# Two small experts in one shared float32 block, and modulation vectors from six wide groups

## Chip, core and metric

The kernel runs on one core of one Trainium2 chip (trn2). The metric is device time in microseconds (us), from the start to the end of one execution; three runs were taken and their median counts. A row says PE for TensorE, PEld for its weight loads, DVE for VectorE, ACT for ScalarE, POOL for GpSimd and SP for SyncE, whose queue issues nearly all transfers here.

## What is computed

One inference step over two transformer layers on 384 tokens: 128 context tokens and 256 latent tokens, width 1024, all in float32. Cut to what matters:

```
shift_a, scale_a, gate_a, shift_f, scale_f, gate_f = split(silu(cond) @ ada_w + ada_b, 6)
h = LN(x) * (1 + scale_a) + shift_a
x = LN1(alpha * x + gate_a * mixers(h))          # attention, short convolution, chunk MLP
h = LN(x) * (1 + scale_f) + shift_f
x = LN2(alpha * x + gate_f * ffn(h))
ffn, layer 0: (silu(h @ w1) * (h @ w3)) @ w2      # d_ff 2816
ffn, layer 1: top 2 of 8 experts, each the same form with d_ff 1408, gated and summed
```

`cond` is one vector for the context tokens and one for the latent tokens, so a modulation vector has two versions. The 6 x 1024 outputs of `ada_w` per layer are counted here in 12 blocks `nb` of 512 columns: 0 to 3 are shift_a and scale_a, 4 and 5 gate_a, 6 to 9 shift_f and scale_f, 10 and 11 gate_f.

Routing the reference's inputs gives 159, 70, 117, 54, 63, 126, 57 and 122 tokens to experts 0 to 7 (768 in all).

## The kernel before

Precision: a product of two float32 matrices is split. Each operand is a high part (`float32r`, cast by ACT) and a rest (`x - high`, subtracted by DVE), and `mm3` issues three fast matmuls: high x high, high x rest, rest x high. A weight block of 1 MB arrives in one of five staging buffers (tag `st`), is cast and subtracted in two halves (`split`, `split2`) into tiles `wh` and `wl`, and the staging buffer is free again once DVE has subtracted. A plain float32 matmul needs no split, and the profile shows it as two records.

Order: all work is recorded by a planner (`Plan`), which gives every instruction a price (`price`), keeps data dependences, buffers and an estimated time for each engine, and writes out the order of each engine; where PE would sit idle for long it inserts filler matmuls (`keep_warm`, line 510; they read only `idr`). All planned instructions carry line 493 or 495 (495: the further matmuls of a bundle that `matmuls` keeps together).

Modulation: `ada_rows` loads 2 MB of `ada_w` for a block `nb` and runs 16 records of 32-row matmuls, four at a time in four column groups of PE, into one PSUM bank, whose four row groups hold partial sums. They are copied into a high part and a rest and summed by matmuls with a 0/1 matrix: `ada_cols` turns them into columns (8 small matmuls with `selc`), `ada_bcast` into rows on all 128 partitions (4 matmuls with `selb`), and `ada_dram` writes two rows to DRAM (2 matmuls with `selc`), from where `spread` broadcasts them by DMA. Start: 4 blocks; mixers of layer 0: 6; dense FFN: 6; mixers of layer 1: 8. In all 48 MB.

Experts (`moe`): expert 7 comes first, since its number is known while routing is not; `order_list` then puts an expert with more than 128 tokens last. `expert` returns ten steps: gate and up matmuls (`up`, in column blocks of 512, 512 and 384), `prep`, `down`, `end`. A block holds up to 128 tokens, gathered by an indirect DMA, transposed on PE and split. Expert 7 and the seven others make eight full blocks. The last one carries a second block of 32 tokens, which is not split and runs in four column groups (`small`). Per full block: 162 matmuls with 512 columns and 48 with 384, and 17.3 MB of weights. `scatter` adds the blocks' results to the tokens, 12 matmuls per block, after the blocks 0 to 2, 3 and 4, and 5 and 6. Tokens beyond these blocks would go to `further` blocks, under a condition at run time, each a whole expert with its loads.

PSUM: eight banks, three tagged `pd` (up matmuls), two `py` (down matmuls, modulation), three `pm`.

## Time and profile before

| | |
|---|---|
| Runs | 1173.18, 1175.70, 1180.41 us; median 1175.7 |
| Profiled execution | 1172.83 us, of which the span from first to last instruction is 1171.1 |
| PE busy | 1133.1 us, 97% of the span |
| DVE, ACT, POOL busy | 827.2, 626.4, 124.3 us |
| Moved by DMA | 282.66 MB, on average 241 GB/s |

A row of a window gives, for a stretch of the span, its length, the busy time of each engine with its number of instructions, the clock granted to PE as a share of full speed, the busy share of the DMA engines and what they moved. PE's busy time comes from modelled ends of pipelined matmuls: of two neighbours the distance of the starts tells the pace, not the length of one. In a timeline, rows of one kind are merged, with their count behind an x.

### The profile page before, as it was taken

To read this page: it belongs to the slowest core of one execution; us is meant where nothing else is said; L and a number is where in the kernel's file an instruction comes from. 1 tells how busy PE (TensorE), PEld (TensorE's weight loads), DVE (VectorE), ACT (ScalarE), POOL (GpSimd) and SP (SyncE) were. 2 spreads that over 40 slices of the span, in tenths; PEclk is the share of its full clock that TensorE was granted. 3 is DMA by queue.
4 is the path that set the end of the run, shared out by engine and by line. 5 is a ranking of instruction groups with operands and counts; after the bars stand their busy time and mean duration, and the time that the engine had idled before them with its cause. 6 is when DMAs were issued, how large, how long until landed. Compare 5 with 4: busy or idle time off the path is not lost. (4 is left out here: it accounts for less than half of the span.)

```text
span 1171.1 us, 15554 instructions
## 1 busy us (share of the span) xinstructions
PE 1133.1 (97%) x5578; PEld 862.3 (74%) x5578; DVE 827.2 (71%) x1391; ACT 626.4 (53%) x997; POOL 124.3 (11%) x141
## 2 busy tenths in 40 slices
PE   8999999999999999989999899999999999999995
PEld 4666668877777878756666677888888888887673
DVE  4475669443535344797568877999999998987855
ACT  4545547431313223264455326878878786885652
POOL 3430003000000000055000110000000000011201
PEclk8999999999999999999999969999999999999998
DMA  9775544573839465354557436999979997996541
GB/s 375 275 267 197 166 142 143 199 269 139 328 110 332 150 238 197 149 185 156 199 186 268 163 130 224 352 362 361 345 294 347 379 361 297 366 343 245 184 176 58
DMA packets 49398, 282.66 MB, mean 241 GB/s; under 512 B 6312, under 2 KB 8104, under 8 KB 21408
## 3 DMA queue, kind: packets, MB, share of 16 engines
q1 hardware_dynamic: 47056, 275.46, 63.7%
q0 software_dynamic: 1392, 4.55, 1.1%
q10 hardware_dynamic: 864, 1.57, 0.4%
q8 instruction: 46, 0.75, 0.3%
q14 instruction: 40, 0.33, 0.1%
HBM read 278.13 MB, written 3.43 MB: 240 GB/s over the span
## 5 line engine op out<-in xcount | busy, mean ns | idle before, releaser
L493 PE MATMUL bank<-q,q 128*128 128x512 f32 (+4 forms) x4111 | 969.6, 389 | 2.6 <-DVE q L493 1.3
L493 PEld LDWEIGHTS bank<-q,q 128*128 128x128 f32 x4111 | 734.4, 189 | 196.4 <-issue 33.6
L493 DVE TENSOR_TENSOR q<-st,q 128x1024 fp32r<-128x1024 f32 x394 | 453.9, 1178 | 113.4 <-ACT q L493 89.0
L493 ACT CAST q<-st 128x1024 fp32r<-128x1024 f32 x394 | 394.0, 1016 | 196.0 <-PE bank L493 101.3
L493 DVE TENSOR_TENSOR q<-bank,q 128x512 fp32r<-128x512 f32 (+5 forms) x117 | 73.0, 635 | 70.6 <-ACT q L493 57.7
L493 DVE TENSOR_TENSOR q<-q,bank 128x512 f32<-128x512 f32 (+3 forms) x111 | 63.8, 584 | 76.7 <-PE bank L493 69.9
L493 ACT CAST q<-bank 128x512 fp32r<-128x512 f32 (+2 forms) x97 | 53.7, 562 | 103.7 <-PE bank L493 94.0
L493 ACT COPY q<-bank 128x128 f32<-128x128 f32 (+3 forms) x184 | 54.5, 350 | 76.3 <-PE bank L493 67.9
L493 PE MATMUL bank<-idf,q 128*128 128x128 f32 (+1 forms) x502 | 81.7, 287 | 12.9 <-ACT q L493 7.4
L493 POOL TENSOR_TENSOR q<-q,nhalf 128x1 f32<-128x1 f32 (+3 forms) x42 | 42.0, 1005 | 473.8 <-DVE q L493 473.7
L493 PEld LDWEIGHTS bank<-idf,q 128*128 128x128 f32 (+1 forms) x502 | 63.2, 147 | 39.5 <-ACT q L493 12.6
L493 POOL TENSOR_TENSOR q<-q,q 128x512 fp32r<-128x512 f32 (+5 forms) x69 | 61.5, 909 | 216.6 <-ACT q L493 155.0
L493 ACT ACTIVATE q<-bank 128x512 f32<-128x512 f32 (+4 forms) x57 | 29.6, 520 | 81.2 <-PE bank L493 74.4
L493 DVE TENSOR_TENSOR q<-q,q 128x512 f32<-128x512 f32 (+13 forms) x131 | 52.3, 420 | 17.4 <-POOL q L493 8.5
L493 PE MATMUL bank<-st,cs 128*32 128x512 f32 x384 | 54.8, 606 | 0.3 <-DMA st<-in_ada_w_dram 0.3
L272 POOL DMA_INDIRECT q<-dr,q x9 | 14.7, 1638 | 346.3 <-DVE q L493 346.3
L493 ACT ACTIVATE q<-bank,q 128x384 f32<-128x384 f32 (+2 forms) x62 | 33.5, 551 | 24.6 <-DVE q L493 21.5
L493 DVE TENSOR_REDUCE q<-bank 128x1 f32<-128x384 f32 (+5 forms) x64 | 24.5, 411 | 20.8 <-PE bank L495 13.5
L493 DVE SCALAR_TENSOR_TENSOR q<-q,q,q 128x512 f32<-128x512 f32 (+1 forms) x43 | 35.5, 882 | 0.1
L510 PE MATMUL bank<-idr 128*128 128x512 f32 x85 | 30.3, 500 | 1.9 <-DVE selt L667 1.7
L495 PE MATMUL bank<-q,q 64*128 64x384 f32 (+2 forms) x76 | 31.7, 515 | 0.0
L493 ACT ACTIVATE q<-bank,q,q 128x128 f32<-128x128 f32 x70 | 26.6, 467 | 4.6 <-DVE q L493 2.8
(90 smaller groups left out, 395.4 us busy)
## 6 DMA issues: line engine op xcount, KB each, us to landing
st<-in_ada_w_dram SPq DMA_DIRECT2D x48, 1024.0 KB
st<-in_moe_w2a_dram SPq DMA_DIRECT2D x40, 1024.0 KB
st<-in_moe_w1a_dram SPq DMA_DIRECT2D x32, 1024.0 KB
st<-in_moe_w3a_dram SPq DMA_DIRECT2D x32, 1024.0 KB
st<-in_ffn_w_dram SPq DMA_DIRECT2D x22, 1024.0 KB
st<-in_w_in_dram SPq DMA_DIRECT2D x16, 1024.0 KB
st<-in_moe_w1b_dram SPq DMA_DIRECT2D x16, 768.0 KB
st<-in_moe_w3b_dram SPq DMA_DIRECT2D x16, 768.0 KB
```

The lines of the kernel that those rows point to most:

```text
L272: self.nc.gpsimd.indirect_dma_start(out=out, out_offset=None, in_=src.rearrange("p t d -> (p t) d"), in_offset=o)
L493: getattr(self.real[o.eng], o.name)(*a, **k)
L495: getattr(self.real[o.eng], o.name)(*[x.real() for x in b], **q)
L510: self.nc.tensor.matmul(z, a, b, start=True, stop=True)
```

## The change

1. The experts other than 7 are sorted by their number of tokens, inside the kernel (`order_list`). Ranks 1 to 4 and then 0 are full blocks as before, so there are six full blocks, not eight. Ranks 5 and 6, the two smallest, share one block (`gather_pair`, `pair`): 64 tokens each, in the two column halves of PE, in plain float32, straight from the staging buffers. Its work is 18 steps (gate and up in halves of the contraction, down in halves), which `PLACES` spreads between the steps of the other blocks, from step 7 to the last block's start. Each half step loads 1 MB (or 0.75 or 0.5) for each of the two experts. `scatter` now runs after the blocks 0 and 1, 2 and 3, 4 and the pair. The loads stay at eight experts.
2. Modulation: four blocks `nb` are done together, in their own column groups, so that a bank holds finished sums and not partial ones: `ada_group` accumulates over eight loads of 1 MB, `ada_out` copies the bank once, transposes it on PE (4 transposes for four blocks) and adds the bias, or adds it to two rows and writes them to DRAM. All gates now come by `spread`. `selc` and `selb` are gone (only the start keeps 8 matmuls with a small 0/1 matrix `selk`). Start: 8 MB as before; mixers of layer 0: 16 MB (12 before); dense FFN: 8 (12 before); mixers of layer 1: 16. In the FFN the bank of a group is held from the second to the fifth column block.
3. Prices of PE in the planner: a fast 512-column matmul from 214 to 232, the smallest fast one from 54 to 112, others by a few ns. `further` gets one more possible block (`MAXX`), and its list is made earlier.

```diff
-MAXX = 5
+MAXX = 6
 W = 32
+
+
+RANKS = (1, 2, 3, 4, 0)
+PAIR = (5, 6)
+H = P // 2
+
+PLACES = (4, 7, 56)
...
-CAPS2 = dict(a4=8, wh=6, wl=6)
-FILL0 = ((0,),(1,),(2,3),())
-GATE = 1
+CAPS2 = dict(a4=10, wh=6, wl=6)
...
-                return 57 if ins[0].dt == F32R else 107
+                return 62 if ins[0].dt == F32R else 109
...
-                return max(54, n * 0.4167 + 1 if n >= 256 else n * 1.6667 + 1)
+                return max(112, n * 0.4453 + 4)
             half = o.cells.shape[0] == 2 or ins[0].cells.shape[0] == 2
-            return max(107, n * (0.85 if half else 1.6667) + 3)
+            return max(214 if len(ins)>1 else 107, n * (0.85 if half else 1.6667) + 6)
...
+    def ada_group(self, l, n, units, zr=None):
+
+
+        nc = self.nc
+        zr = zr or self.bank([512], name="zrows", tag="py")
+        for u in units:
+            w = self.load(self.A["ada_w"][l, n, u], 4, 512)
+            split = (l, n) == (0, 0)
+            first, last = (u % 4 == 0, u % 4 == 3) if split else (u == 0, u == KC - 1)
+            k = [4 * (j % 2) + u % 4 if split else u for j in range(4)]
+            nc.matmuls([(zr[32 * j : 32 * j + 32, :], self.cs[:, k[j], :], w[:, j, :], dict(start=first, stop=last, tile_position=(0, 32 * j))) for j in range(4)])
+        return zr
...
+    def ada_out(self, l, n, zr, cols, rows):
+
+        nc = self.nc
+        if cols:
+            e = self.m2([512], name="ae")
+            nc.any.copy(e, zr)
+            pt = self.bank([4, P], name="zcols")
+            for c in range(4):
+                nc.tensor.transpose(pt[:, c, :], e[:, 128 * c : 128 * c + 128], self.idf)
+            for j, (out, one) in cols.items():
+                nb = 4 * n + j
+                b = self.abc[:, l, 4 * nb : 4 * nb + 4][:, :, None].to_broadcast([P, 4, 2])
+                nc.vector.scalar_tensor_tensor(out, pt[:, :, 32 * j : 32 * j + 2], one, b, op0=ALU.add, op1=ALU.add)
+        if rows:
+            b = self.m2([512], name="mrow")
+            for j, one in rows.items():
+                r, nb = slice(32 * j, 32 * j + 2), 4 * n + j
+                nc.sync.dma_start(b[r], self.A["ada_b"][l : l + 1, 512 * nb : 512 * nb + 512].to_broadcast([2, 512]))
+                nc.vector.scalar_tensor_tensor(b[r], zr[r], one, b[r], op0=ALU.add, op1=ALU.add)
+                nc.sync.dma_start(self.mod[l][0:2, nb, :], b[r])
...
-        gate = lambda: [self.ada_bcast(l, 4 + nb, 0.0) for nb in range(2)]
         fill(3)
-        if GATE == 1:
-            ga = [self.ada_bcast(l, 4 + nb, 0.0) for nb in range(2)]
-            gate = lambda: ga
+        ga = [[self.spread(l, 4 + nb, m) for m in range(2)] for nb in range(2)]
...
-            if n == 2:
-                gf[0] = self.ada_bcast(l, 10, 0.0)
-            elif n == 3:
-                gf[1] = self.ada_bcast(l, 11, 0.0)
+            if n == 4:
+                gf = [[self.spread(l, 10 + nb, m) for m in range(2)] for nb in range(2)]
...
+        key = sm([Q], "key")
+        nc.vector.scalar_tensor_tensor(key, cnt[:, 0:Q], -float(NE), self.ie[:, 0, 0:Q], op0=ALU.mult, op1=ALU.add)
+        before, place = sq("before"), sq("place")
+        wide = lambda v: v[:, None, :].to_broadcast([P, Q, Q])
+        tall = lambda v: v[:, :, None].to_broadcast([P, Q, Q])
+
+        nc.vector.tensor_tensor(before, wide(key), tall(key), op=ALU.is_lt)
+        rank = sm([Q], "rank")
+        nc.vector.tensor_reduce(rank, before, axis=AX.X, op=ALU.add)
...
+        self.done = done = self.m2([NE], name="done", tag="s", hold=True)
+        last, first = sm([Q], "islast"), sm([Q], "isfirst")
+        nc.vector.tensor_scalar(first, rank, 0.0, float(W), op0=ALU.is_equal, op1=ALU.mult)
+        nc.vector.tensor_scalar(last, rank, PAIR[0] - 0.5, float(H - P), op0=ALU.is_gt, op1=ALU.mult)
+        nc.vector.memset(done, float(P))
+        nc.vector.scalar_tensor_tensor(done[:, 0:Q], first, float(P), last, op0=ALU.add, op1=ALU.add)
...
+    def gather_pair(self, cols):
+
+        nc = self.nc
+        ph = [self.m2([P], F32R, "ph") for t in range(NT)]
+        for t in range(NT):
+            for i in range(2):
+                nc.vector.tensor_scalar(ph[t][:, H * i : H * i + H], self.iot[:, 0:H], cols[i][t], None, op0=ALU.is_equal)
+        x = self.rows_of(ph, P)
+        xw = self.m2([KC, P], name="xp", tag="a4")
+        for g in range(2):
+            pt = self.bank([4, P], name="zgat")
+            for j in range(4):
+                nc.tensor.transpose(pt[:, j, :], x[:, 512 * g + 128 * j : 512 * g + 128 * j + 128], self.idf)
+            nc.any.copy(xw[:, 4 * g : 4 * g + 4], pt)
+        return xw, ph
...
+        def up(gi, fw, w, u):
+
+            zz = self.bank([fw], name="zp" + w, tag="pd")
+            st = [self.load(src(w, gi, u), 4, fw) for src in srcs]
+            for k in range(4):
+                nc.matmuls([(zz[r], s["x"][:, 4 * u + k, r], st[i][:, k], dict(start=(k == 0), stop=(k == 3), tile_position=(0, H * i))) for i, r in enumerate(halves)])
+            if u == 0:
+                s["z"] = self.m2([fw], name="zh")
+                nc.any.copy(s["z"], zz)
+                return
+            z = s["z"]
+            nc.vector.tensor_add(z, z, zz)
+            if w == "w1":
+                s[gi] = self.silu(z, fw)
+                return
+            g, nf = s[gi], fw // 128
+            nc.any.mul(g, g, z)
+            pt = self.bank([nf, P], name="zgT")
+            for f in range(nf):
+                nc.tensor.transpose(pt[:, f, :], g[:, 128 * f : 128 * f + 128], self.idf)
+            s[gi] = self.m2([nf, P], name="gp")
+            nc.any.copy(s[gi], pt)
+
+        def down(gi, nf, u):
+            fs = range(2 * u, min(2 * u + 2, nf))
+            y = [self.bank([512], name="zyp", tag="pd") for nb in range(2)]
+            st = [self.load(src("w2", gi, u), len(fs), 1024) for src in srcs]
+            for f in fs:
+                for nb in range(2):
+                    k = dict(start=(f == fs[0]), stop=(f == fs[-1]))
+                    nc.matmuls([(y[nb][r], s[gi][:, f, r], st[i][:, f - fs[0], 512 * nb : 512 * nb + 512], dict(k, tile_position=(0, H * i))) for i, r in enumerate(halves)])
+            if gi + u == 0:
+                s["y"] = self.m2([2, 512], name="yp", tag="a4")
+                s["y"] = [s["y"][:, nb] for nb in range(2)]
+            for nb in range(2):
+                if gi + u == 0:
+                    nc.any.copy(s["y"][nb], y[nb])
+                else:
+                    nc.vector.tensor_add(s["y"][nb], s["y"][nb], y[nb])
...
+        work = []
+        for gi, fw in enumerate((512, 512, 384)):
+            work += [lambda gi=gi, fw=fw, w=w, u=u: up(gi, fw, w, u) for w in ("w1", "w3") for u in range(2)]
+            work += [lambda gi=gi, fw=fw, u=u: down(gi, fw // 128, u) for u in range(2)]
+        a, b, c = PLACES
+        return [(a, start)] + [(b + (c - b) * i // (len(work) - 1), f) for i, f in enumerate(work)] + [(c, end)]
...
-                if i % 2 == 0 and i:
-                    self.scatter(ys, ya, i == 2)
+                if i in (1, 3, n - 1):
+                    self.scatter(ys, ya, i == 1)
                     ys.clear()
-                    if i == 6:
+                    if i == n - 1:
...
-        for j in range(7):
-            e = self.expert([block(j)], srcs(j), then(j))
-            nxt = [gat(j + 1), gat(8)] if j == 6 else [gat(j + 1)]
+        for j in range(n):
+            e = self.expert([block(j)], ranked(RANKS[j - 1]) if j else lambda w, gi, u: self.wsrc(NE - 1, w, gi, u), then(j))
+            nxt = [gat(j + 1), gat(n + 1)] if j == n - 1 else [gat(j + 1)]
             steps += e[:AHEAD] + nxt + e[AHEAD:]
-        steps += self.expert([block(7), block(8)], srcs(7), then(7), gf)
+        steps += self.expert([block(n), block(n + 1)], ranked(RANKS[n - 1]), then(n), gf)
+        pair = self.pair(lambda: self.gather_pair([col(self.posp, r) for r in PAIR]), lambda: [[a[:, r] for a in self.gatep2] for r in PAIR], [ranked(r) for r in PAIR], ys.append)
+        for at, f in reversed(pair):
+            steps.insert(at, ("", f))
...
+                n, us = 1 + i // 2, range(4 * (i % 2), 4 * (i % 2) + 4)
+                z[n] = self.ada_group(l, n, us, z.get(n))
...
+        z0 = [None]
 
         def fill1(g):
             if 1 <= g <= 4:
-                self.ada_cols(1, g - 1, (sh[0], sh[1], sc[0], sc[1])[g - 1], 0.0 if g < 3 else 1.0)
+                z0[0] = self.ada_group(1, 0, (2 * g - 2, 2 * g - 1), z0[0])
+            if g == 4:
+                self.ada_out(1, 0, z0[0], {0: (sh[0], 0.0), 1: (sh[1], 0.0), 2: (sc[0], 1.0), 3: (sc[1], 1.0)}, {})```

On PE, in the dense FFN of layer 0 around the first modulation block of layer 1. Before: `cs` is silu of the conditioning vectors, `q...` beside `selc` the high part and the rest of the sums, the other rows are the FFN's own:

```order
L493 MATMUL bank3_2594<-st4_2257,cs_88 32x512 x4
L493 MATMUL bank3_2594<-st1_2260,cs_88 32x512 x4
L493 MATMUL bank5_2608<-q43_2563,q411_1952 128x512
...
L493 MATMUL bank3_2630<-selc_79,q210_2610 128x2
L493 MATMUL bank3_2630<-selc_79,q28_2618 128x2
...
L493 MATMUL bank4_2622<-q418_2454,q23_2521 128x512
```

Now, from the second quarter of the group (bank4_2518) on; `bank3_2876`, `bank3_2908` and `bank3_2926` are the down products of three neighbouring outputs, `bank5_2900` is a gate product of the next column block:

```order
L498 MATMUL bank4_2518<-st2_2538,cs_84 32x512
L500 MATMUL bank4_2518<-st2_2538,cs_84 32x512 x3
L498 MATMUL bank4_2518<-st3_2558,cs_84 32x512
L500 MATMUL bank4_2518<-st3_2558,cs_84 32x512 x3
L498 MATMUL bank3_2876<-q43_2711,q20_2790 128x512
...
L498 MATMUL bank5_2900<-q417_2831,q411_1866 128x512
L498 MATMUL bank5_2900<-q46_2842,q411_1866 128x512
L498 MATMUL bank5_2900<-q417_2831,q412_1875 128x512
L498 MATMUL bank5_2900<-q417_2831,q411_1866 128x512
L498 MATMUL bank3_2908<-q43_2711,q20_2790 128x512
...
L498 MATMUL bank3_2926<-q43_2711,q22_2827 128x512
```

The small matmuls are gone, bank 4 stays with the group, and the down products, 12 matmuls each, follow each other in bank 3 alone, with four matmuls of the next block between two of them.

On PE, in the first expert block, between the last down products of its first column block (`bank4_6340`, `bank7_6483` is the next up product) the pair's first step stands, two matmuls of 64 rows side by side for each of four slices:

```order
L498 MATMUL bank4_6340<-q43_6303,q215_6289 128x512
L498 MATMUL bank6_6416<-st1_6182,q426_6257 64x512
L500 MATMUL bank6_6416<-st0_6206,q426_6257 64x512
L498 MATMUL bank6_6416<-st1_6182,q426_6257 64x512
L500 MATMUL bank6_6416<-st0_6206,q426_6257 64x512
...
L498 MATMUL bank7_6483<-q47_6313,q423_6130 128x512
```

Before, the two neighbours followed each other:

```order
L493 MATMUL bank3_6592<-q45_6687,q220_6728 128x512
L493 MATMUL bank7_6784<-q416_6696,q424_6413 128x384
```

On SP, at the same place in the queue of loads. Before, expert 0's second half of the down weights is followed by the loads of the next expert alone:

```order
L493 DMA st1_6749<-in_moe_w2b_dram 128x1024
L493 DMA st4_6765<-in_moe_w3a_dram 128x2048
L493 DMA st0_6790<-in_moe_w3a_dram 128x2048
L493 DMA st2_6819<-in_moe_w1a_dram 128x2048
L493 DMA st3_6847<-in_moe_w1a_dram 128x2048
L493 DMA st1_6874<-in_moe_w2a_dram 128x2048
```

Now loads of the pair stand between them, two for each step:

```order
L498 DMA st2_6765<-in_moe_w2b_dram 128x1024
L498 DMA st1_6777<-in_moe_w3a_dram 128x2048
L498 DMA st4_6803<-in_moe_w3a_dram 128x2048
L498 DMA st0_6823<-in_moe_w3a_dram 128x2048
L498 DMA st3_6837<-in_moe_w3a_dram 128x2048
L498 DMA st2_6869<-in_moe_w2a_dram 128x2048
L498 DMA st1_6889<-in_moe_w2a_dram 128x2048
```

The same five buffers now serve both. All rows of the pair on PE form 35 separate pieces between rows of the full width.

## Rows read from the trace of the kernel before

**Rows 1.** The page: the span, the busy time of each engine, and what DMA moved in 40 equal slices of the span.

```profile
span 1171.1 us, 15554 instructions
...
PE 1133.1 (97%) x5578; PEld 862.3 (74%) x5578; DVE 827.2 (71%) x1391; ACT 626.4 (53%) x997; POOL 124.3 (11%) x141
...
GB/s 375 275 267 197 166 142 143 199 269 139 328 110 332 150 238 197 149 185 156 199 186 268 163 130 224 352 362 361 345 294 347 379 361 297 366 343 245 184 176 58
```

**Rows 2.** Windows: the mixers of layer 0, the dense FFN, the mixers of layer 1, routing, the first seven expert blocks, the last block and the close. Columns: length, busy us (number) of each engine, PE clock, DMA share, GB/s.

```profile
80.00:200.00 120.00, 118.44 (x635) 81.46 (x634) 84.98 (x183) 66.91 (x178) 14.22 (x19) 1.00 0.46 163
200.00:480.00 280.00, 279.95 (x1348) 221.71 (x1348) 128.18 (x159) 90.08 (x114) 4.05 (x3) 1.00 0.60 218
540.00:660.00 120.00, 120.00 (x626) 79.05 (x625) 80.83 (x176) 57.55 (x157) 14.71 (x18) 1.00 0.59 213
660.00:706.00 46.00, 38.26 (x162) 32.26 (x160) 36.10 (x128) 12.52 (x19) 7.01 (x8) 0.74 0.35 132
706.00:1061.00 355.00, 353.29 (x1708) 298.58 (x1707) 323.48 (x428) 280.87 (x330) 13.62 (x8) 1.00 0.89 335
1061.00:1171.00 110.00, 95.63 (x500) 63.50 (x498) 75.01 (x92) 52.66 (x71) 16.96 (x14) 0.95 0.45 164
```

**Rows 3.** Timeline of SP's queue: start us, time over which the issues of the row stretch, what. The first is the second up load of expert 7, the next three the first w3 loads of the second, third and fourth block's period, the last one is for the last block and runs ahead of it.

```profile
694.88 17.23 SPq L493 DMA_DIRECT2D st<-in_moe_w3a_dram  x2
...
743.28 3.32 SPq L493 DMA_DIRECT2D st<-in_moe_w3a_dram  x2
...
792.36 3.25 SPq L493 DMA_DIRECT2D st<-in_moe_w3a_dram  x2
...
841.33 5.34 SPq L493 DMA_DIRECT2D st<-in_moe_w3a_dram  x2
...
1053.33 8.63 SPq L493 DMA_DIRECT2D st<-in_moe_w3a_dram  x2
```

**Rows 4.** Timeline of PE in the dense FFN: start us, length, what. `st,cs` are the modulation matmuls of one block `nb`, `selc` the small ones, `idf` transposes, `q,q` fast matmuls.

```profile
244.35 0.60 PE L493 MATMUL bank<-idf,q 128*128 128x128 f32 x4
244.70 5.82 PE L493 MATMUL bank<-q,q 128*128 128x512 f32 x24
250.35 0.60 PE L493 MATMUL bank<-idf,q 128*128 128x128 f32 x4
...
255.28 1.92 PE L493 MATMUL bank<-st,cs 128*32 128x512 f32 x16
257.13 0.51 PE L493 MATMUL bank<-q,q 128*128 128x512 f32 x1
...
258.84 0.95 PE L493 MATMUL bank<-selc,q 128*128 128x2 f32 x8
259.65 2.55 PE L493 MATMUL bank<-q,q 128*128 128x512 f32 x10
```

**Rows 5.** Timeline of PE in the attention of layer 1: two plain float32 matmuls (lines 493 and 495) in the two column halves of PE, two records each.

```profile
606.72 0.59 PE L493 MATMUL bank<-q,q 128*64 128x512 f32 x1
606.72 0.59 PE L495 MATMUL bank<-q,q 128*64 128x512 f32 x1
607.15 0.59 PE L493 MATMUL bank<-q,q 128*64 128x512 f32 x1
607.15 0.59 PE L495 MATMUL bank<-q,q 128*64 128x512 f32 x1
```

**Rows 6.** Timeline of PE in the last block: pieces of the 32-token block (`st,q`, four column groups) between fast matmuls of the full width.

```profile
1102.12 1.92 PE L493 MATMUL bank<-st,q 128*32 128x512 f32 x16
1103.97 5.82 PE L493 MATMUL bank<-q,q 128*128 128x512 f32 x24
1109.72 1.92 PE L493 MATMUL bank<-st,q 128*32 128x512 f32 x16
...
1118.24 1.50 PE L493 MATMUL bank<-st,q 128*32 128x384 f32 x16
1119.66 0.96 PE L493 MATMUL bank<-q,q 128*128 128x384 f32 x4
```

**Rows 7.** Windows in the expert blocks, columns as in Rows 2.

```profile
760.00:780.00 20.00, 20.00 (x99) 16.47 (x98) 18.27 (x22) 15.83 (x21) 1.68 (x1) 1.00 0.98 394
755.00:804.00 49.00, 49.00 (x240) 41.64 (x239) 45.27 (x50) 39.57 (x47) 1.68 (x1) 1.00 0.95 364
```

**Rows 8.** Who waited for whom, SP's queue: us in total, times, longest us.

```profile
SPq L493 <- DVE q L493: 726.0, 208, 34.8
```

**Rows 9.** Groups of instructions by line, engine and form: count, busy us, mean ns of one, idle time before them.

```profile
L493 DVE TENSOR_TENSOR q<-q,bank 128x512 f32<-128x512 f32 x73 | 49.6, 684 | 61.3 <-PE bank L493 61.2
...
L493 PE MATMUL bank<-selc,q 128*128 128x2 f32 x128 | 16.6, 239 | 2.0 <-ACT q L493 1.1 <-DVE q L493 0.9
...
L272 POOL DMA_INDIRECT q<-dr,q x9 | 14.7, 1638 | 346.3 <-DVE q L493 346.3
...
L493 PE MATMUL bank<-q,selb 128*128 128x512 f32 x24 | 7.6, 399 | 0.0
...
L493 PE MATMUL bank<-q,selc 128*2 128x512 f32 x12 | 4.6, 400 | 1.5 <-DVE q L493 1.5
```

**Rows 10.** Timeline of PE at the start: the small matmuls of the second modulation block of the first half, the first of them with the high part, the next with the rest.

```profile
22.31 0.27 PE L493 MATMUL bank<-selc,q 128*128 128x2 f32 x1 [0.28 <-ACT q L493]
23.04 0.94 PE L493 MATMUL bank<-selc,q 128*128 128x2 f32 x7 [0.46 <-DVE q L493]
```

More of the change, by code (lines that the diff above doesn't have):

```diff
@@ L746, in ada_cols @@
-    def ada_cols(self, l, nb, out, one):
-        nc = self.nc
-        eh, el = self.ada_rows(l, nb)
-        pc = self.bank([4, 2], name="zcols", tag="py")
-        for j in range(4):
-            s = slice(128 * j, 128 * j + 128)
-            nc.tensor.matmul(pc[:, j, :], eh[:, s], self.selc, start=True, stop=False)
-            nc.tensor.matmul(pc[:, j, :], el[:, s], self.selc, start=False, stop=True)
-        b = self.abc[:, l, 4 * nb : 4 * nb + 4][:, :, None].to_broadcast([P, 4, 2])
-        nc.vector.scalar_tensor_tensor(out, pc, one, b, op0=ALU.add, op1=ALU.add)
-        return eh, el
@@ new lines, in ada_group, with ada_start @@
+        return zr
+    def ada_start(self, g, sh, sc):
+        nc = self.nc
+        zr = self.ada_group(0, 0, range(4 * g, 4 * g + 4))
+        e = self.m2([512], name="ae")
+        nc.any.copy(e, zr)
+        pc = self.bank([4, 2, 2], name="zcols", tag="py")
+        for c in range(4):
+            nc.tensor.matmul(pc[:, c].rearrange("p i m -> p (i m)"), e[:, 128 * c : 128 * c + 128], self.selk, start=True, stop=True)
+        for i, (out, one) in enumerate(((sh, 0.0), (sc, 1.0))):
+            nb = 2 * i + g
+            b = self.abc[:, 0, 4 * nb : 4 * nb + 4][:, :, None].to_broadcast([P, 4, 2])
+            nc.vector.scalar_tensor_tensor(out, pc[:, :, i, :], one, b, op0=ALU.add, op1=ALU.add)
@@ L1742, in lead @@
         for nb in range(2):
[L1743 removed]
+            gf.append([self.spread(1, 10 + nb, m, hold=True) for m in range(2)])
         for t in range(NT):
```

224 lines of the change are left out of this document (97 added, 127 removed).

## The prediction

> **What bounds the kernel now.** First the page: PE is busy for 97% of the span, DVE for 71%, and DMA moves from 58 to 379 GB/s in the slices [rows 1]. An average over unlike stages proves little, so next the windows by stage. In the mixers of both layers and in the dense FFN PE is busy for 118.44 of 120, 279.95 of 280 and 120.00 of 120 us, with DMA at a share of 0.46 to 0.60: there PE alone bounds. In the stretch of the first seven expert blocks, 355 us, PE has 353.29 us, but DVE also 323.48 (91%) and DMA a share of 0.89 at 335 GB/s: three resources nearly full, and only routing has PE waiting for long [rows 2].
>
> Is a "busy" PE at its pace? 24 fast matmuls of 512 columns take from 244.70 to 250.35, 0.235 us each [rows 4], and the blocks repeat with that pace: the first w3 loads of three blocks stand at 743.28, 792.36 and 841.33, so a full block takes 49.08 or 48.97 us where no scatter falls into it [rows 3]; 162 matmuls at 0.235 and 48 narrower ones fill that. So in the blocks PE ends last, with DMA close behind. Work taken from PE counts in full until DMA becomes the limit.
>
> **The change, part by part.** *Two full blocks fewer.* 49.08 + 48.97 = 98.0 us of PE [rows 3]. Scatter: seven blocks of 12 matmuls become five and the pair, 12 x 0.235 = 2.8 us less [rows 4]. Removed: 100.8 us.
>
> *The pair.* By the code, 32 up and 22 down matmuls of 512 columns for each half, and 16 of 384. The same form runs in attention: the matmuls of the two halves start together, and the next two records start 0.43 us later; a plain float32 matmul is two records, so two side by side take 0.86 us [rows 5]. 54 x 0.86 = 46.4 us. For 384 columns the 32-token block gives the ratio: 1118.24 to 1119.66 against 1102.12 to 1103.97, 1.42 to 1.85 [rows 6], so 0.66 each and 16 x 0.66 = 10.6. Transposes of tokens and gated values: 19 at 0.35/4 = 0.09, and 12 small matmuls at (259.65 - 258.84)/8 = 0.10 [rows 4]: 2.9 us. Together 59.9.
>
> *Changing between halves and full width.* The 18 steps stand in 35 pieces. A piece of the 32-token block takes 1.85 us, of which four steps at 0.43 are 1.72 [rows 5, 6]; the 24 full matmuls behind it take 5.75 us until the next piece, and 5.65 where no change is near [rows 4, 6]. So a piece costs 0.13 + 0.10 = 0.23 us more than its matmuls, and 35 of them 8 us. The Trainium skill, "TensorEngine Tiling (Array Packing)", section Tiling Modes, says that a change of the tiling mode drains TensorE, without a price. It speaks against spreading the pair so finely. The trace agrees: with the rule the pieces cost 8 us, without it nothing.
>
> PE in this stretch: 100.8 - 59.9 - 8 = 33 us less; 41 if the pieces cost nothing.
>
> *Does DMA follow?* The weights are the same: 335 GB/s x 355 us = 118.9 MB [rows 2]. In 355 - 33 = 322 us that is 369 GB/s. DMA has given 364 over a whole block at a share of 0.95, and 394 over 20 us at 0.98 [rows 7]; at 364 the stretch takes 327 us. Nothing shows 369 held for 300 us. From below: at no more than today's mean it would stay at 355, less the w3 load of the last block issued ahead at 1053.33 (two loads, 2 MB, 6 us) [rows 3], so a gain of 6. I take 364, thus 5 us lost and 28 won, because what holds the loads back today is DVE: SP's queue waited for it 726 us in all, each time for a staging buffer [rows 8], and DVE loses the subtractions of two experts of eight, while the pair's steps free their buffers without it.
>
> *Lists and gathers.* The rank list and the pair's sums in SBUF are DVE and ACT work beside PE, and DVE gets free what two blocks took; I price them at nothing, as long as the list is not later than now. SP waits for it: of the two w3 loads of the first block the second is issued 17 us after the first, at 711.8 [rows 3]. Now the pair's first two loads stand ahead of both w3 loads, so four loads follow the wait, 4 x 2.8 us at 375 GB/s: they land near 723 or a little later. PE reaches the w3 matmuls after 96 fast matmuls (22.6 us from 706) and a pair step (3.4 us), near 732. Covered by 9 us; if not, the PE waits by what is missing.
>
> *Modulation.* The big matmuls stay: 16 records, 1.85 us per block of columns (255.28 to 257.13), and 8 small ones cost 0.81 us [rows 4]; the groups counted by form are 128 small ones, 24 with `selb` and 12 with `selc` as weights [rows 9].
> - Mixers of layer 0: off 4 x 0.81 + 8 x 0.235 = 5.1; on two more blocks 3.7 and 8 transposes 0.7. Gain 0.7.
> - FFN: off 5.1 and two blocks 3.7; on 4 transposes 0.35. Gain 8.5. But one of two down banks is held by the group through three column blocks: between two down products stand four other matmuls, 0.94 us, while DVE's add alone takes 0.684 [rows 9]. The signals there and back must fit into 0.26 us. 15 such places, 0 to 0.15 us each: I take 1 us off. Gain 7.5.
> - Mixers of layer 1: off 4 x 0.81 + 12 x 0.235 + 8 x 0.235 = 7.9, on 0.7. Gain 7.2.
> - Start: two chains per half become one, without the subtraction; the small matmuls with the rest start 0.73 us after the first and take 0.94 [rows 10]. About 1 us for each of two halves, 2; bounds 0 and 4.
>
> These stages are PE's [rows 2], so I take them in full: 17.4 us. The lower end, half, is for places where the softmax chain and not PE ends last. The gates' way through DRAM is hidden: they are written before the third part of the mixers and read after it. Work behind 1061 (last block, close) stays as it is.
>
> *Prices.* They move instructions everywhere. No row prices this; routing has 7.7 us without PE work at a clock of 0.74 [rows 2], so I allow 5 us either way and take nothing.
>
> **Sum.** 28 + 17.4 = 45.4 us. The profiled execution of 1172.8 us becomes 1127.4; the median of the runs lies 2.9 above it, so 1130.
>
> **Rivals.**
> 1. *DMA becomes the bound.* The blocks save only 6 us: 23.4 in all, 1152. For it: a share of 0.89 already, and a pair step holds two of five staging buffers until PE reaches it. Against: 394 GB/s at the same buffers [rows 7]. Chance 0.22.
> 2. *Modulation gives nothing.* The down bank costs a whole add with its signals, 15 x 0.8 = 12 us, and the mixers give half: 28.5 in all, 1147. For it: 0.26 us is little for two signals. Against: the four matmuls are there in the order. Chance 0.09.
> 3. *Slower: the halves run in turn.* If the two experts' matmuls don't overlap, the pair takes 57 us more, and the end comes at 1130 + 57 = 1187. It decides from where 45.4 of the 57 us (80%) of one half are not hidden. Against: common starts and a common pace in attention [rows 5]; there both read operands that had long been in SBUF, here two fresh loads. Chance 0.04.
> 4. *It doesn't do what it says.* Should ranks 5 and 6 hold over 64 tokens, or rank 0 over 160, a whole further block runs behind everything: 49 us and more, at least 1179. The reference's inputs give 57, 54 and 159, and nine gathers in the trace (eight blocks and the 32 tokens) show none today [rows 9]. Chance 0.03.
>
> **From these the numbers.** My forecast has 0.62. Its own range: 8 us of pieces and 5 of DMA that may not come, 2 more at the start and 5 of order on one side (1175.7 - 65 = 1111), 12 less on the other (1142). With rivals 1 and 2 and a few us on them the range reaches to 1156 and leaves out under 0.1. About 1% (12 us) can be told from no change here. Faster by more than that: the forecast, rival 2 and most of rival 1, 0.88. Within 1%: the rest of rival 1, 0.05. Slower: rivals 3 and 4, 0.07.
>
> **What would show it.** After the change the seven experts' stretch, from the first fast expert matmul to the first matmul of the 32 tokens, should last about 327 us, with 364 GB/s and a DMA share over 0.95; rival 1 has 349 us at about 335 to 340. The pair's two lines should start together, 0.43 us from record to record; rival 3 has them one after the other. A lone piece should cost about 0.2 us more than its matmuls. FFN and mixers of layer 1 should be 7 to 8 us shorter each, with PE still full; rival 2 shows PE waiting for DVE in the FFN. Eight gathers and no further block. I am wrong in the mechanism if DVE is again over 90% busy in the blocks, or if PE waits there for loads while DMA's share is below 0.9: then the five buffers, not the rate, are the limit.

## The result, and the profile after the change

The changed kernel takes 1130.74 us (median of 4 runs, 1128.24 to 1131.56), the kernel before 1176.62 beside it: a ratio of 0.962, 95% interval [0.959, 0.965]. A second measurement of the same kernel gave 1132.21 us and 0.964 [0.962, 0.966]. The profiled execution took 1130.28 us, its span 1128.5. 1130 was predicted, but it is luck that two errors cancel in that sum, as the stages show.

The page after the change, to be read against [rows 1]:

```profile
span 1128.5 us, 14587 instructions
...
PE 1083.0 (96%) x5256; PEld 771.3 (68%) x5256; DVE 737.1 (65%) x1296; ACT 537.7 (48%) x900; POOL 123.8 (11%) x141
...
GB/s 369 311 276 287 193 188 139 197 211 162 238 172 272 150 288 139 222 221 157 118 246 241 204 125 224 321 359 381 332 340 373 389 386 357 341 360 265 212 175 59
```

Windows of the changed kernel, columns as in [rows 2]: dense FFN, attention of layer 1, routing, the experts up to the first 32-token matmul, last block and close.

```profile
200.00:470.00 270.00, 268.97 (x1242) 210.81 (x1242) 120.25 (x146) 86.66 (x107) 2.67 (x3) 1.00 0.58 207
540.00:640.00 100.00, 98.23 (x510) 64.67 (x510) 68.41 (x157) 48.97 (x145) 6.97 (x11) 1.00 0.62 220
646.91:679.59 32.68, 27.29 (x130) 22.24 (x129) 29.59 (x113) 10.61 (x17) 5.87 (x7) 0.78 0.36 128
679.59:1018.36 338.77, 331.53 (x1534) 234.63 (x1534) 244.99 (x362) 201.66 (x253) 8.24 (x7) 0.99 0.90 349
1018.36:1128.50 110.14, 95.73 (x499) 63.52 (x498) 79.25 (x95) 55.27 (x73) 18.90 (x15) 0.96 0.47 173
```

In the experts' stretch DVE fell from 91% [rows 2] to 245 of 339 us, 72%, and the same weights moved at 349 GB/s. PE is idle for 7.2 us there, and its clock is not always full.

Landmarks on PE's timeline cut both spans alike: second row of fast matmuls (30.25 before, 28.63 now), last paired matmul of layer 0's attention, first and last one of layer 1's, first fast expert matmul, first 32-token matmul, end.

| Stage | before | after | won | forecast |
|---|---|---|---|---|
| Start | 30.25 | 28.63 | 1.6 | 2 |
| Mixers of layer 0, to the last pair | 140.14 | 137.10 | 3.0 | 0.7 |
| From there to the first pair of layer 1 (dense FFN in it) | 400.25 | 392.40 | 7.9 | 7.5 |
| Attention of layer 1 | 75.85 | 69.10 | 6.7 | 7.2 |
| Output projection and routing | 59.54 | 52.36 | 7.2 | 0 ± 5 |
| Experts, to the first 32-token matmul | 355.1 | 338.8 | 16.3 | 28 |
| Last block and close | 110.0 | 110.1 | -0.1 | 0 |

The sum is 42.6, the difference of the spans. The two stages that are far off are routing, 7 us unforeseen, and the experts, 12 us short. The experiments are about these.

A window's clock is a mean over two levels, 2.4 and 1.2 GHz, and work at the lower one takes twice as long (a filler 0.50 us in place of 0.24, in the last section), so a window of length L and clock c loses L x (1 - c), or less where PE also waits in it. In routing that is up to 46 x 0.26 = 12.0 us before [rows 2] and 32.68 x 0.22 = 7.2 us in this profile: some 4.8 of the 7.2 us won there are time at the lower clock. In the experts' stretch, these are the only two 6-us windows of the stretch below 0.95:

```profile
679.59:685.59 6.00, 6.00 (x22) 4.81 (x23) 2.70 (x5) 2.44 (x3) 0.96 (x1) 0.77 0.31 90
769.59:775.59 6.00, 4.02 (x16) 3.62 (x17) 4.22 (x5) 3.62 (x6) 0.00 (x0) 0.72 0.99 413
```

They lose 6 x 0.23 + 6 x 0.28 = 3.1 us, the first as an inheritance from routing, the second behind 2 us without work while PE waited for a gather. Thus 338.8 = 7.2 idle + 3.1 clock + 328.5 of work at full clock, the "rest". The same for each kernel that ran (pieces are the separate places of the pair on PE; the rest can still hold waits that the modelled ends of matmuls hide):

| Kernel | stretch | PE idle | clock | rest | GB/s | pieces |
|---|---|---|---|---|---|---|
| before | 355.1 | 1.7 | 0 | 353.4 | 335 | |
| modulation alone | 356.7 | 3.1 | 0 | 353.6 | 333 | |
| before, new prices | 384.7 | 21.7 | 8.4 | 354.6 | 312 | |
| changed | 338.8 | 7.2 | 3.1 | 328.5 | 349 | 35 |
| changed, again | 339.2 | 7.1 | 2.9 | 329.2 | 349 | 35 |
| changed, old prices | 341.3 | 11.1 | 1.7 | 328.5 | 346 | 33 |
| full width | 324.0 | 6.7 | 1.7 | 315.6 | 365 | 0 |
| one load | 332.8 | 8.1 | 0.5 | 324.1 | 307 | 34 |
| full width, one load | 335.9 | 12.4 | 10.7 | 312.8 | 304 | 0 |
| thin pair | 325.4 | 20.9 | 8.1 | 296.4 | 363 | 22 |
| bundled | 332.4 | 8.6 | 2.8 | 321.0 | 355 | 18 |
| bundled, in twos | 332.2 | 7.2 | 0.6 | 324.4 | 358 | 17 |
| merged | 357.1 | 14.4 | 2.9 | 339.8 | 330 | 9 |
| bundled, six buffers | 327.3 | 7.9 | 1.7 | 317.8 | 364 | 18 |

### The profile page after: what moved, and what is told of

It reads as the page before. It is cut to its first block, busy times and chain, and to the rows that moved or that the text cites. A ratio compares the mean times of both kernels' runs of the same rounds, so it can differ in the third digit from the quotient of the medians.

```text
span 1128.5 us, 14587 instructions
## 1 busy us (share of the span) xinstructions
PE 1083.0 (96%) x5256; PEld 771.3 (68%) x5256; DVE 737.1 (65%) x1296; ACT 537.7 (48%) x900; POOL 123.8 (11%) x141
## 3 DMA queue, kind: packets, MB, share of 16 engines
q0 software_dynamic: 1248, 4.02, 1.0%
## 5 line engine op out<-in xcount | busy, mean ns | idle before, releaser
L498 PE MATMUL bank<-q,q 128*128 128x512 f32 (+6 forms) x3679 | 875.8, 391 | 4.2 <-DVE q L498 2.4
L498 PEld LDWEIGHTS bank<-q,q 128*128 128x128 f32 (+2 forms) x3679 | 654.5, 189 | 203.9 <-issue 34.4
L498 DVE TENSOR_TENSOR q<-st,q 128x1024 fp32r<-128x1024 f32 (+1 forms) x324 | 373.7, 1184 | 118.6 <-ACT q L498 94.3
L498 ACT CAST q<-st 128x1024 fp32r<-128x1024 f32 (+1 forms) x324 | 318.7, 1018 | 231.0 <-PE bank L498 124.6
L498 DVE TENSOR_TENSOR q<-q,bank 128x512 f32<-128x512 f32 (+3 forms) x121 | 70.5, 592 | 114.9 <-PE bank L498 108.2
L498 ACT COPY q<-bank 128x128 f32<-128x128 f32 (+2 forms) x201 | 64.1, 370 | 88.6 <-PE bank L498 61.3
L498 PE MATMUL bank<-idf,q 128*128 128x128 f32 (+1 forms) x503 | 82.3, 287 | 24.1 <-ACT q L498 10.5
L498 PEld LDWEIGHTS bank<-idf,q 128*128 128x128 f32 (+1 forms) x503 | 59.4, 145 | 63.5 <-ACT q L498 18.8
L498 POOL TENSOR_TENSOR q<-q,nhalf 128x1 f32<-128x1 f32 (+3 forms) x42 | 41.5, 995 | 461.3 <-DVE q L498 461.3
L498 POOL TENSOR_TENSOR q<-q,q 128x512 fp32r<-128x512 f32 (+4 forms) x70 | 66.9, 972 | 220.7 <-ACT q L498 140.9
L498 ACT CAST q<-bank 128x512 fp32r<-128x512 f32 (+2 forms) x58 | 31.7, 554 | 110.4 <-PE bank L498 105.0
L498 PE MATMUL bank<-st,q 128*64 128x512 f32 (+3 forms) x280 | 84.1, 578 | 0.0
L498 DVE TENSOR_TENSOR q<-bank,q 128x512 fp32r<-128x512 f32 (+5 forms) x83 | 50.4, 616 | 44.5 <-ACT q L498 38.9
L500 PE MATMUL bank<-st,q 128*64 128x512 f32 (+1 forms) x140 | 64.2, 581 | 0.0
L498 DVE TENSOR_TENSOR q<-q,q 128x512 f32<-128x512 f32 (+13 forms) x135 | 54.5, 426 | 13.6 <-POOL q L498 10.7
L498 ACT ACTIVATE q<-bank 128x512 f32<-128x512 f32 (+4 forms) x51 | 26.2, 514 | 66.3 <-PE bank L498 57.9
L498 PE MATMUL bank<-st,cs 128*32 128x512 f32 x96 | 47.5, 609 | 1.1 <-DMA st<-in_ada_w_dram 0.8
L500 PE MATMUL bank<-st,cs 128*32 128x512 f32 x288 | 47.9, 609 | 0.0
L498 ACT ACTIVATE q<-bank,q 128x384 f32<-128x384 f32 (+2 forms) x58 | 30.9, 537 | 29.3 <-DVE q L498 22.8
L498 PEld LDWEIGHTS bank<-st,q 128*64 128x64 f32 (+1 forms) x280 | 20.2, 122 | 33.9 <-issue 33.4
L498 DVE SCALAR_TENSOR_TENSOR q<-q,q,q 128x512 f32<-128x512 f32 (+2 forms) x45 | 41.0, 966 | 0.1
```

The lines of the kernel that those rows point to most:

```text
L498: getattr(self.real[o.eng], o.name)(*a, **k)
L500: getattr(self.real[o.eng], o.name)(*[x.real() if isinstance(x, View) else x for x in b], **q)
```

## The experiments

**Full width.** The pair's half matmuls become whole ones:

```diff
-nc.matmuls([(zz[r], s["x"][:, 4 * u + k, r], st[i][:, k], dict(..., tile_position=(0, H * i))) for i, r in enumerate(halves)])
+nc.tensor.matmul(zz, s["x"][:, 4 * u + k, :], st[k % 2][:, k], start=(k == 0), stop=(k == 3))
```

> The changed kernel with one edit: the pair's matmuls run in the full width of PE (all 128 columns, alternately on the one and on the other expert's load) and not in two halves. It leaves out half of the pair's products, so its output is not the reference's; the loads, the number of plain float32 passes (54 x 0.86 and 16 x 0.66 us) and the places of the steps stay. In the changed kernel the experts' stretch, from the first fast expert matmul to the first matmul of the 32 tokens, lasts 338.8 us: 7 us with PE idle and 332 busy, 11 more busy than I had priced. Theory A, the changes between halves and full width cost more than my 0.23 us for each of 35 pieces: without them the stretch falls by about 17 to 20 us, to 319 to 322. Theory B, loads come late and the modelled ends of the matmuls hide PE's waiting for them: nothing changes in the loads, so the stretch stays above 335.

Measured: 324.0 us, 1117.8 in all (one run). Theory A: the rest fell by 12.9 us with the same loads and the same passes. At one place the two traces stand beside each other. PE's timeline in the changed kernel, from the start of a pair step over 24 fast matmuls to the next step:

```profile
708.65 0.64 PE L498 MATMUL bank<-st,q 128*64 128x512 f32 x1
708.65 0.64 PE L500 MATMUL bank<-st,q 128*64 128x512 f32 x1
709.13 0.59 PE L498 MATMUL bank<-st,q 128*64 128x512 f32 x1
...
712.23 5.87 PE L498 MATMUL bank<-q,q 128*128 128x512 f32 x24
718.03 0.64 PE L498 MATMUL bank<-st,q 128*64 128x512 f32 x1
```

and in the full-width kernel:

```profile
708.40 3.60 PE L498 MATMUL bank<-st,q 128*128 128x512 f32 x8
711.43 6.13 PE L498 MATMUL bank<-q,q 128*128 128x512 f32 x24
717.40 1.88 PE L498 MATMUL bank<-st,q 128*128 128x512 f32 x4
```

9.38 us against 9.00: 0.38 for this piece, and 12.9/35 = 0.37 on the mean, where I had 0.23. The mean takes all 12.9 us for pieces; what the rest holds of waits may differ between the two. The halves start together and follow each other by 0.43 us, as in [rows 5]; the first of a piece takes 0.48.

**One load.** Both halves use the first expert's weights: `st = [self.load(srcs[0](w, gi, u), 4, fw)] * 2`.

> The changed kernel with one edit: each step of the pair loads only the first expert's weights and both halves multiply with them. It leaves out the second expert of the pair, so its output is not the reference's; 17.3 MB of 118.6 are not loaded, PE's work is the same. Theory A (changes of mode cost the 11 us): only idle time of PE can go, so the stretch of 338.8 us falls by at most 7, to 332 or a little more. Theory B (late loads): the stretch falls to about 322, and ScalarE's waits for loads, 60 us in all now, mostly vanish.

Measured: 332.8 us, 1129.2 in all (one run; its routing ended later). Theory B's 322 is refuted: with 16 MB less and PE's matmuls the same, 6 us go, though ACT's waits for loads fell from 60 to 21 us. They do not go from idle time, as theory A had said, but 4.4 from the rest and 2.6 from the clock. So about 4 us of the changed kernel's rest depend on the loads, or on the plan, which changes with them (34 pieces).

**Thin pair.** `for k in range(4)` becomes `range(1)`, and `for f in fs` becomes `fs[:1]`.

> The changed kernel with one edit: the pair's up steps multiply only the first of their four slices, its down steps only the first of their two; all loads stay. It leaves out most of the pair's products, so its output is not the reference's. PE has 24 x 0.86 + 12 x 0.66 + 10 x 0.86 = 37 us less to do in the stretch of 338.8 us. If PE alone bounds (theory A): about 302 us, with 118.6 MB at 393 GB/s. If the rate of DMA bounds (theory B): no shorter than 326 us at 364 GB/s. If the five staging buffers bound: longer than 326 us with a DMA share under 0.9.

Measured: 325.4 us at 363 GB/s, 1121.1 in all (one run). This is theory B's number, that of the loads and not of PE: with 37 us of matmuls taken away, only 13 are won, and PE is idle for 21 us and at a lower clock behind that. The window of the stretch:

```profile
681.23:1006.63 325.40, 304.51 (x1373) 228.19 (x1373) 242.94 (x360) 198.91 (x253) 9.98 (x9) 0.98 0.93 363
```

So with five buffers the loads take some 325 us whatever PE does, near my 327, and the changed kernel lies 13 us above that. Whether the rate alone sets these 325 us is not shown: the DMA share is 0.93, but SP's queue still waits 60.8 us for PE to free the pair's buffers.

**Old prices.** The four lines of `price` as before.

> The changed kernel with the planner's prices of PE as they were before; modulation and the pair stay. Routing, from the end of the output projection of layer 1 to the first fast expert matmul, took 42.4 us before and takes 32.7 now, which I had not forecast. Theory P, the corrected prices make the planner place the first tile's norm and the fillers better: with the old prices routing takes 40 to 43 us again and the whole kernel is 6 to 10 us slower than the changed one (ratio to before about 0.968). Rival M, the rebuilt modulation did it (no small matmuls, no rows to write, and its banks free at that place): routing stays at 32 to 34 us and the ratio at 0.962.

Measured: 1138.39 us, 0.971 [0.967, 0.975]; routing from 638.58 to 682.00, 43.4 us. Theory P by its numbers, but not by its reason: the output projection ended 8 us earlier, and the experts began only 2.4 later. The prices move PE's work from one stage into another. Of the 6 to 8 us between the medians the first profile of the changed kernel places 2.5 in the stretch and 2.4 ahead of it; the second one (below) begins its experts at 685.51, later than here, so the 2.4 are no more than one execution differs from the next.

**Modulation alone.** The kernel before with `ada_group`, `ada_start`, `ada_out` and `spread` of the changed one.

> The kernel before with only the modulation rebuilt: experts, lists and prices as before. The first fast expert matmul stood at 706.0 us before and stands at 679.6 now (26.4 us earlier); with old prices and the pair it stood at 682.0. Theory M, modulation alone brings the 24 us: it stands at 681 to 683, and the kernel takes about 1152 us (ratio about 0.980). By my prediction, 17.4 us: at 688 to 689, 1158 us, and the rest would belong to the rank list or the prices.

Measured: 1145.61 us, 0.974 [0.970, 0.978]; first expert matmul at 678.39, 27.6 us earlier. More than theory M asked, with old prices and no rank list: the gain ahead of the experts is the modulation's. ACT's timeline shows a part of the unforeseen one, the norm of the first tile in routing (ACTIVATE). In the kernel before PE's output projection ended at 663.60, in this one at 639.35:

```profile
671.81 1.52 ACT L493 ACTIVATE q<-q,q,q 128x512 f32<-128x512 f32 x2 [6.97 <-DVE q L493]
```

```profile
641.44 1.52 ACT L498 ACTIVATE q<-q,q,q 128x512 f32<-128x512 f32 x2 [0.46 <-DVE q L498]
```

8.2 us behind the projection before, 2.1 now. Before, the norm waited for DVE for 7 us; now the planner has the first tile's statistics done earlier. With old prices and the pair, thus with the same new modulation, it was late again; with new prices alone, thus with the old modulation, it was early:

```profile
648.46 1.52 ACT L498 ACTIVATE q<-q,q,q 128x512 f32<-128x512 f32 x2 [8.63 <-DVE q L498]
```

```profile
673.79 1.52 ACT L493 ACTIVATE q<-q,q,q 128x512 f32<-128x512 f32 x2 [0.96 <-DVE q L493]
```

9.9 us behind the projection (638.58) and 2.2 (671.59). Projection and routing together took 59.65 us in the one and 55.41 in the other, 59.54 before and 54.27 with modulation alone. So what routing gains goes with this order, and the order is a property of one plan, not of the new modulation or the new prices.

**New prices alone.** The kernel before with the new lines of `price`.

> The kernel before with only the planner's new prices. Between the changed kernel with old prices and with new ones the first fast expert matmul moved from 682.0 to 679.6 and the stretch from 341.3 to 338.8; the ratio to before was 0.971 against 0.962. Theory P, the prices are worth 3 to 10 us by themselves: the same here, 1166 to 1173 us. Rival, they only suit the new order: within 3 us of before.

Measured: 1201.35 us, 1.023 [1.017, 1.028], slower by 2.3%. Both theories are wrong. The experts began at 706.11, as before, so the prices bring nothing ahead of them. The stretch grew by 29.6 us, and its work at full clock stayed (354.6 against 353.4). PE's waits in it:

```profile
PE bank L493 <- DMA q<-dr,q: 20.7, 6, 4.4
PE bank L493 <- DVE q L493: 1.0, 1, 1.0
```

The six waits are for the gathered tokens (`dr`), 4.4 us the longest, and 8.4 us of low clock go with them: under these prices the planner asks for the gathers too late (the second block's was issued at 769.97, and PE waited for it until 779.63). So the corrected prices are no gain by themselves.

**Bundled.** A pair step becomes one bundle (down steps likewise):

```diff
-            for k in range(4):
-                nc.matmuls([(zz[r], ...) for i, r in enumerate(halves)])
+            nc.matmuls([(zz[r], ...) for k in range(4) for i, r in enumerate(halves)])
```

> The changed kernel with one edit: all matmuls of a step of the pair are recorded as one bundle, which the planner cannot split, so that the pair stands in 18 pieces on PE and not in 35; what is computed, the loads and the matmuls are the same. Without any change between halves and full width the stretch fell by 14.8 us (338.8 to 324.0), 0.42 us for each of 35 pieces. Theory A (each change of width costs): 17 pieces fewer bring 7 us, the stretch lasts about 331.5 and the kernel about 1123 us (ratio to before about 0.955). Rival C, the two halves themselves run slower than their 0.86 us, whatever stands between them: the stretch stays at 338 to 339.

Measured: stretch 332.4 us, theory A's number; rival C is refuted. In all 1129.15, 0.961 [0.958, 0.964], hardly faster: in the profile routing ended at 684.0 in place of 679.6, with the same order of PE up to there, and last block and close took 2.4 us more.

**Bundled, in twos.** The positions of two neighbouring steps made equal, `(i // 2 * 2)` for `i`.

> As the bundled kernel, and the 18 steps stand in twos at nine places, so that their four loads of 1 MB come close together. The pieces are about as many (17). Theory A alone: as the bundled one, about 331 us of stretch. If the five staging buffers matter (four of them held by the pair at a time, so the full blocks' loads come late): longer than the bundled one, 334 us or more, with more waiting of ScalarE for loads.

Measured: 332.2 us, 1129.06 in all, 0.961 [0.957, 0.964]. No difference in the stretch, but its rest is 3.4 us above the bundled kernel's with one piece fewer: the rest carries some 3 us that pieces do not explain. Where the planner may put fast work between two steps, it does.

**The changed kernel again.**

> The changed kernel once more, unedited, on the chip of the two next runs. Kernels whose order up to the experts is the same had their first fast expert matmul at 679.6, 679.7, 681.2, 683.9 and 684.0 us, while TensorE ran at its lower clock for a shorter or a longer part of routing. If that is the clock alone and not the edits, this one falls anywhere between 679 and 685 too, while its stretch of experts lasts 338 to 340 us as before.

Measured: 0.964 [0.962, 0.966]; experts from 685.51, stretch 339.2. The stretch repeats within 0.4 us, what lies ahead of it does not, and the profile behind the stage table is the one with the earlier experts. Windows of the attention of layer 1, first the profile above, then this one:

```profile
590.00:630.00 40.00, 39.07 (x211) 24.46 (x208) 29.59 (x68) 20.13 (x57) 2.61 (x4) 1.00 0.82 278
```

```profile
590.00:630.00 40.00, 38.24 (x202) 23.63 (x200) 28.26 (x66) 18.56 (x55) 2.74 (x5) 0.96 0.71 253
```

The same code lost 1.6 us to the clock here. Projection and routing:

```profile
631.04:685.51 54.47, 47.54 (x214) 38.56 (x212) 46.73 (x140) 17.44 (x24) 9.07 (x9) 0.83 0.35 119
```

Of the 7.2 us won there 5.1 stay in this execution, with up to 54.47 x 0.17 = 9.3 us lost to the clock against 7.2 in the first. Without the clock's part both executions have 45.2 us, and the kernel before 47.5: what both keep of the 7.2 us is some 2.

**Merged.** Nine pieces: 16 matmuls of both contraction halves in one bundle, four loads awaited together.

> The changed kernel with the pair's half steps put together: one bundle of 16 matmuls for each product over the whole width of 1024, or over all slices of the down weights, so nine pieces on PE and no sums of halves; the four loads of a step (1 MB each, five buffers) are waited for together. What is computed and loaded is the same. Theory A (about 0.4 us for each piece): 26 pieces fewer than 35 bring 10 us, the stretch lasts about 328 us, total about 1120 (ratio about 0.955). Rival D (the five buffers): while four of them wait for the pair, the full blocks' loads stop; ScalarE's waits for loads grow and the stretch lasts 335 us or more.

Measured: 357.1 us, 1155.54 in all, 0.986 [0.984, 0.988]. Rival D, and worse than it said. The groups by form in the stretch show where PE's busy time went:

```profile
L515 PE MATMUL bank<-idr 128*128 128x512 f32 x77 | 22.3, 403 | 0.0
```

77 filler matmuls, 22.3 us, stand there; the changed kernel has two. 34 of them run directly ahead of a piece of the pair, where the plan has PE wait for its four loads, the others ahead of the full blocks' matmuls. ACT waits 32.0 us for the first half of w3, 7.7 in the changed kernel. That the pair's four of five buffers hold these loads back is argued from that. Pieces are cheap against starved loads.

**Full width and one load.**

> Both edits that left something out, together: the pair in full width (no change of width) and only one of its two loads used and made. It leaves out half of the pair's products and takes the rest with wrong weights, so its output is not the reference's. Alone they brought 14.8 us (338.8 to 324.0) and 6.0 us (to 332.8). If they are two separate costs, pieces and late loads: about 318 us, near the 314 that PE's matmuls alone take by my prices. If the full-width kernel had already all that PE can give: 323 to 324.

Measured: 335.9 us (one run), neither theory's number. The rest is 312.8, near the 314 of pure matmuls, but PE was idle for 12.4 us and lost 10.7 to the clock behind it. The edits do not add; that another plan, made for fewer loads, is the reason is not shown.

**Six buffers.** The bundled kernel with `st=6` and `a4=10` in place of 5 and 12.

> The bundled kernel (18 pieces) with six staging buffers of 1 MB in place of five, for which two of the twelve 4 KB tiles a4 are given up; what is computed and loaded is the same. Bundled, the stretch lasts 332.4 us: 321 of PE's work at full clock, 8.6 with PE idle and 2.8 lost to a lower clock after it, with loads coming late on ScalarE and a DMA share of 0.91 at 355 GB/s. If the five buffers hold back the loads: DMA's rate goes to 365 GB/s or more and the stretch to about 323 to 326, total about 1120 to 1124. If the rate is the limit, or the gathers and not the weight loads are what PE waits for: 331 to 333 as now.

Measured: 327.3 us at 364 GB/s, between the two forecasts and nearer the buffers'; 1124.93 in all, 0.958 [0.956, 0.961]. This version beats both kernels, the changed one by 5.8 and 7.3 us in its two measurements (on other chips; 0.958 against 0.962 and 0.964 of the kernel before). The idle time is 0.7 us less than in the bundled kernel and the rest 3.1 us less, with the same 18 pieces. The window:

```profile
681.94:1009.29 327.35, 319.50 (x1531) 235.22 (x1531) 243.88 (x361) 202.33 (x253) 11.87 (x9) 0.99 0.93 364
```

## Why the prediction was right, and where it was not

The total came true since the stages ahead of the experts gave 9 us more than forecast and the experts 12 less. That is luck: in the second profile the same stages gave 20.5 us, 3 more than the 17.4 forecast.

- **Removed and added matmuls.** Right. Without changes of width the rest should be 353.4 - 100.8 + 59.9 = 312.5 us; the full-width kernels have 315.6 and 312.8. The halves share PE as in [rows 5]; rival 3 is refuted, and eight gathers without a further block refute rival 4.
- **Changing between halves and full width.** The step that failed: "a piece costs 0.13 + 0.10 = 0.23 us", 8 us in all. It was 0.37 on the mean, 13 us. I had taken it from whole pieces of the 32-token block between long runs of fast matmuls [rows 6]. 13 of the 35 pieces are followed by transposes, which I had priced like any other. PE's timeline:

```profile
863.08 0.59 PE L498 MATMUL bank<-st,q 128*64 128x512 f32 x1
...
863.61 0.66 PE L498 MATMUL bank<-idf,q 128*128 128x128 f32 x4
864.19 0.64 PE L498 MATMUL bank<-st,q 128*64 128x512 f32 x1
...
864.67 0.59 PE L498 MATMUL bank<-st,q 128*64 128x512 f32 x1
```

  The record ahead of the transposes takes 0.53 and not 0.43 us, they themselves 0.58 and not 0.35, the record behind them 0.48: 0.38 us for splitting one step. In the full-width kernel four transposes at such a place take 0.43 (855.57 to 856.00), so 0.30 of the 0.38 belong to the change of width:

```profile
855.57 0.60 PE L498 MATMUL bank<-idf,q 128*128 128x128 f32 x4
856.00 1.88 PE L498 MATMUL bank<-st,q 128*128 128x512 f32 x4
```

  The rule of the Trainium skill, "TensorEngine Tiling (Array Packing)", section Tiling Modes, that a change of mode drains TensorE, agrees with that; the price comes from these rows.
- **What is left in the rest.** PE's work shrank by 24.9 us, not 33. Pieces explain 5 of the 8; one load makes some 4 more depend on the loads, and a sixth buffer takes 3.1 off the rest with the pieces unchanged. That these are hidden waits is argued, not shown.
- **Lists and gathers.** I had priced them at nothing. PE's waits in the stretch:

```profile
PE bank L498 <- DMA q<-dr,q: 3.4, 4, 2.1
PE bank L498 <- DVE q L498: 2.5, 5, 0.9
PE bank L498 <- ACT q L498: 1.1, 1, 1.1
```

  Before, gathers had 0.9 us of them. The longest one here is followed by the window at 0.72, so gathers cost some 4 us more with the clock behind them.
- **Does DMA follow?** The time that the loads need was right (325 us at 363 GB/s with much less PE work), but the kernel does not reach it: 349 GB/s, and 8.6 us of new idle time and low clock where I had 5 for DMA (some 4 of the 8.6 are the gathers', 1.4 the clock inherited from routing). None of PE's waits is for a weight load by the profile. I had written that PE waiting for loads at a share below 0.9 would mean the five buffers. The share is 0.90, and ACT waits for weights:

```profile
ACT q L498 <- DMA st<-in_moe_w1b_dram: 22.6, 6, 7.3
ACT q L498 <- DMA st<-in_moe_w1a_dram: 17.6, 9, 5.9
```

  My reason for 364 GB/s had a gap. The 726 us of [rows 8] are those of the whole span; in the stretch SP's queue waited for DVE 283.2 us before and 171.7 now. But the pair's buffers come free only when PE reaches its steps, and SP now waits for that, most in the changed kernel, then bundled, then with six buffers (L500 holds the second matmul of each two side by side):

```profile
SPq L498 <- PE bank L500: 73.7, 16, 7.9
SPq L498 <- PE bank L500: 69.1, 17, 6.8
SPq L498 <- PE bank L500: 39.3, 16, 6.0
```

  A sixth buffer (with two `a4` tiles fewer) brings the bundled kernel 5 us and 9 GB/s, so the buffers act. No kernel moved more than 365 GB/s over the stretch; that the rate acts beside them is argued. Part of rival 1 came true: 338.8 lies midway between its 349 and my 327. DVE let go, as forecast.
- **Modulation.** Too small in the sum. With it rebuilt the experts begin 27.6 us earlier alone, 24.0 with old prices and the pair, 26.4 and 20.5 in the two profiles of the changed kernel; I had 17.4. Attention of layer 1 came near its 7.2 (6.7, and 4.3 in the second profile). That the FFN's stage came within 0.5 us of its 7.5 is luck: under old prices it won 14.7 us, in modulation alone (385.56 us) as with the pair (385.58), and the new prices took 7 of these back. Why it is 14.7 no run shows. Rival 2's stall did not show, PE has 268.97 of 270 us in the FFN.
- **Prices, and routing.** "No row prices this" was honest, but 0 ± 5 was wrong in place: of the 7.2 us in routing some 4.8 are the clock of one execution, and what is left goes with DVE's order, which turned early under the new modulation alone and under new prices alone, and late under old prices with the pair. The prices by themselves cost 2.3%, and with the new code they bring 6 to 8 us. Why the planner's order turns as it does stays open.

## What to carry to other kernels

When a small block is spread between larger ones, count the places where PE changes width, transposes included, and price one from a trace with the same neighbours. Before joining pieces, count the buffers that a joined piece holds: nine pieces, with PE and ACT waiting for loads, were 25 us slower than 18. Give a planner's prices and a new code a run each, since their effects do not add. Split a good total by stages, since errors may cancel in it, and profile the same kernel twice before a stage's few microseconds are explained.

## What the runs showed of the hardware

The same program lost up to 7.2 us to the clock in routing in one execution and up to 9.3 in projection and routing in another, with 1.6 more in the attention before. Seven profiles here with the same order of PE's work up to the experts began them between 679.59 and 685.51 us. Fillers show the two levels, PE's timeline in routing of the changed kernel:

```profile
646.91 1.55 PE L515 MATMUL bank<-idr 128*128 128x512 f32 x6
...
654.94 2.05 PE L515 MATMUL bank<-idr 128*128 128x512 f32 x4
656.94 1.81 PE L498 MATMUL bank<-idf,q 128*128 128x128 f32 x8
```

The four end 2.00 us after they start, 0.50 each, where 20 of them took 4.73 us in the kernel before (663.60), 0.24 each. There the fillers that are to keep PE's clock up run at the lower level themselves, ahead of transposes for which routing waits. In the stretch an idle time of 2.05 us was followed by a clock of 0.72 over 6 us, so a short wait can cost more than its length; in the bundled kernel a wait of 1.82 us for the same gather was followed by full clock.
